# A split between streamed and gathered value columns, moved from 1536 and 512 to 1408 and 640

## The chip, the cores and the metric

The kernel runs on one core of one Trainium2 chip. The metric is the device time of one execution, in microseconds (us).

## What is computed

The kernel is one layer of a decoder: a mixer (a gated recurrence and a convolution side by side) and then an expert layer. The change lies in the second half of the expert layer. There are 256 tokens of width 2048 and 16384 experts, each with a row of `u_table` and a row of `v_table`. Each token has chosen 128 experts (8 heads, 16 each).

```python
u = jnp.take(u_table, ib, axis=0)
act = jnp.einsum('cd,chkd->chk', hb, u)
w = gb * jax.nn.gelu(act)
v = jnp.take(v_table, ib, axis=0)
out = jnp.einsum('chk,chkd->cd', w, v)     # (tokens, 2048)
x = x + gt2[:, None, :] * rms_norm(out, g_post_ffn[l])
```

## The kernel before

The stages follow one another: the mixer, the scores and the first expert product, a short stage that turns the chosen experts into a dense matrix of weights `S` (16384 experts by 256 tokens), and from about 1305 us the value stage, in which `out` is formed.

The 2048 columns of `v_table` are formed in two ways. The first `DV` = 1536 columns are streamed for all experts: the loop over `r` = 0 to 127 takes 128 experts at a time, and `vload` (L1080) loads their 128 x 1536 value rows on SP's queue into one of the three buffers of `vfR`. For float32 precision each operand is split into a high and a low part: `split` (L94) copies on ScalarE (L95, the high part) and subtracts on VectorE (L96, the low part). The high parts go round three buffers (`vHr`), the low parts round two (`vLr`). The load buffer is free again once the low part is formed. `wsplit` (L1050) splits the weights of the next row in the same way, 128 x 256. `vmul` (L1087) then runs 3 products x 2 token halves x 3 blocks of 512 columns, so 18 matmuls a row, into six banks of PSUM.

The last `GV` = 512 columns are gathered for the chosen experts alone: there are 256 units (token half, choice), and for each of them `vgather` (L1062) issues on GpSimd's queue an indirect DMA of 128 rows of 512 columns; `vadd` (L1069) multiplies by the token's weight and adds to `og` on VectorE (L1074; the first of a token half is L1072). A gather buffer returns to the list `gvs` when its addition is issued, and the freed buffer is then gathered into again. The list starts with four buffers (two each in the slots `h2` and `l2`); at rows 7 and 15 the weight rows already used give four more each. Additions start at row 3 (`VLAG`): three a row up to row 8, then two.

VectorE's order in this loop is the written one: `vload`'s low split, `wsplit`'s, then the additions. The other engines' instructions are ordered by the scheduler, with loads and splits moved ahead of their places (`HPV`). SP's queue and GpSimd's queue run in order, as each engine does.

The stage before it (L921 to L1038) shares the area `R` of 28 KB a partition with the value stage's buffers. `trs` and two of the `rawR` buffers lie in it from 10 to 16 KB; `gated` (L968) reads `trs` up to the end of the scores, `weigh` (L990) and `sides` up to the end of that stage. Of the three load buffers, given out from the top down, the first two lie above what these use, the third over it. After the last row the two token halves are normalised, scaled, added to `x1` and written, in four blocks of 512 columns (L1140 to L1162).

Of the kernel before, what the change touches and what calls it, by code (L numbers as in the profile page):

```python
# [11 lines left out]
F32 = mybir.dt.float32  # L12
F32R = mybir.dt.float32r
# [5 lines left out]
PSUM = bass.MemoryType.PSUM  # L19
DRAM = bass.MemoryType.DRAM  # L20

T = 256
D = 2048
# [22 lines left out]
RB = 8  # L46
QPARTS = ((0, 6), (6, 12), (12, 16))
MANV = {mybir.EngineType.DVE}
RKB = 28
# [20 lines left out]
KU = DU // 128  # L70
GU = D - DU
KSL = (6, 6, 4)
DV = 1536
GV = D - DV
UPARTS = ((0, 6), (6, 12))

PCOLS = {}
# [10 lines left out]
def build(nc, tc, A, stop=None):  # L88
    ctx = ExitStack()
    pool = lambda name, bufs=1, **kw: tc.tile_pool(name=name, bufs=bufs, **kw)  # L90
# [45 lines left out]
    def slot(tag, kb, dt=F32):  # L136
        return slots.tile([128, kb * 256], dt, tag=tag, name=f"s{tag}")
# [44 lines left out]
    sb = Area(0, 12, slot("b", 12, F32R))  # L182
# [205 lines left out]
    for j in range(4):  # L388
        n = 0
# [229 lines left out]
    def flat(a, n):  # L619

        return Sf[:, a * T:(a + n) * T]
# [4 lines left out]

    UW = UPARTS[0][1]
    ua = Area(0, RKB - 9)
    sb = Area(0, 12, slot("b", 12, F32R))
# [79 lines left out]
    asked = [False]  # L709
# [93 lines left out]
    def upiece():  # L803
        if "parts" not in state or not state["parts"]:
            state["r"] = r = urows.pop(0)
            state["parts"] = list(UPARTS)
            state["ps"] = accum()
# [13 lines left out]
    with tc.manual_schedule(engines={mybir.EngineType.DVE}):  # L821
        for h in range(NH):
            if h != 1:
                n = 4 if h == 0 else 2
# [41 lines left out]
    xa = Area(tk0, tk1)  # L866
# [32 lines left out]
    pp = psM.enter_context(pool("ppM", space=PSUM))  # L899
    pG = psM.enter_context(pool("pG", 3, space=PSUM))  # L900
    pW = psM.enter_context(pool("pW", 3, space=PSUM))
    va = Area(0, 10)
    wn = va.t(2, NK)
    og = va.t(2, GV)
    jk2 = va.t(128, dt=BF)
    ss = [va.t(4) for _ in range(2)]
    AtR = Area(0, 4, slot("l2", 4)).ring(8, 128)
    xa = Area(10, RKB)
    vfR = Ring([xa.t(DV) for _ in range(3)][::-1])
    BtR = Area(0, 6, slot("h0", 6)).ring(3, 4, 128)  # L910
    ba = Area(0, 6, slot("h1", 6))
    wts = [[ba.t(128) for _ in range(3)] for tt in range(2)]
# [3 lines left out]
    la = [Area(0, 6, slot(x, 6)) for x in ("l0", "l1")]  # L916
    mr = Ring([x.t(1024) for x in la])
    xiR = Ring([x.t(4, 128) for x in la])
    xoR = Ring([og[:, i, :] for i in range(2)])

    def turn():  # L921

        for tt in range(2):
            for q in range(0, KT, 4):
                xi, xo = xiR(), xoR()
                nc.sync.dma_start(xi, x1t[:, q:q + 4, tt * 128:tt * 128 + 128])
                ps = pm.tile([128, 512], F32, name="pm")
                for i in range(4):
                    nc.tensor.transpose(ps[:, 128 * i:128 * i + 128], xi[:, i, :], ident)
                nc.scalar.activation(xo, ps, AF.Copy)  # L930
                nc.sync.dma_start(x1d[tt, :, 128 * q:128 * q + 512], xo)
                yield

    turns = turn()
    mst = va.t(512)
    mods = modfull(5, lambda: pp.tile([128, 512], F32, name="modps"), lambda: pm.tile([128, 512], F32, name="pm"), mr,
                   lambda: mst, 1024, nc.sync, KSPL)

# [92 lines left out]
    for _ in mods:  # L1031
# [6 lines left out]
    psM.close()  # L1038
    vctx = ExitStack()
    pm = vctx.enter_context(pool("pmV", space=PSUM))  # L1040
    out = [[vctx.enter_context(pool(f"po{i}{n}", space=PSUM)).tile([128, 512], F32, name=f"o{i}{n}")
            for n in range(DV // 512)] for i in range(2)]


    units = [(tt, s_) for tt in range(2) for s_ in range(NK)]
    sb = Area(0, 12, slot("b", 12, F32R))
    vHr = Ring([slot("l0", 6, F32R), sb.t(DV), slot("h0", 6, F32R)])
    vLr = Ring([slot("l1", 6, F32R), slot("h1", 6, F32R)])
    WR = sb.ring(3, 2, T)
    def wsplit(r, a=0, b=T):  # L1050
        ww = WR() if a == 0 else wlast.pop(0)
        if b < T:
            wlast.append(ww)
        with tc.high_priority(offset=HPV):
            split(ww[:, 0, a:b], ww[:, 1, a:b], srow(r)[:, a:b])
        return ww[:, 0, :], ww[:, 1, :]

    wlast = []

    gvs, asked = [v for x in ("h2", "l2") for v in Area(0, 4, slot(x, 4)).ring(2, GV).aps], []  # L1060

    def vgather():  # L1062
        tt, s_ = units.pop(0)
        g = gvs.pop(0)
        nc.gpsimd.indirect_dma_start(out=g, out_offset=None, in_=A["vg"],  # L1065
                                     in_offset=bass.IndirectOffsetOnAxis(ap=ei[:, tt, s_:s_ + 1], axis=0))
        asked.append((g, tt, s_))

    def vadd():  # L1069
        g, tt, s_ = asked.pop(0)  # L1070
        if s_ == 0:
            nc.vector.tensor_scalar(og[:, tt, :], g, wn[:, tt, s_:s_ + 1], None, op0=OP.mult)  # L1072
        else:
            nc.vector.scalar_tensor_tensor(og[:, tt, :], g, wn[:, tt, s_:s_ + 1], og[:, tt, :], op0=OP.mult, op1=OP.add)  # L1074
        gvs.append(g)
# [4 lines left out]
    def vload(r, eng=None):  # L1080
        v, vh, vl = vfR(), vHr(), vLr()
        with tc.high_priority(offset=HPV):
            nc.sync.dma_start(v, A["vd"][r])
            split(vh, vl, v, eng)
        return vh, vl

    def vmul(r, w, v, tts=(0, 1), ns=range(DV // 512)):  # L1087
        (wh, wl), (vh, vl) = w, v
        for a, b in ((wh, vh), (wl, vh), (wh, vl)):
            for tt in tts:  # L1090
                for n in ns:
                    nc.tensor.matmul(out[tt][n], a[:, tt * 128:tt * 128 + 128],  # L1092
                                     b[:, 512 * n:512 * n + 512], start=r == 0 and a is wh and b is vh,
                                     stop=r == NK - 1 and b is vl)


# [2 lines left out]
    with tc.high_priority(offset=HPW):  # L1099
        ws = [wsplit(r, 0, 128) for r in range(2)]  # L1100
        for r in range(2):
            vmul(r, ws[r], vs[r], (0,))
    with tc.manual_schedule(engines=MANV):
        for r in range(2):
            wsplit(r, 128)
        wnext = wsplit(2)
        for r in range(NK):
            if r < 2:
                vmul(r, ws[r], vs[r], (1,))
            else:  # L1110
                v, w = vload(r), wnext
                if r < NK - 1:
                    wnext = wsplit(r + 1)
                if r < NK - 2:
                    vmul(r, w, v)
                else:
                    vs[r - NK], ws[r - NK] = v, w
                if r == NK - 1:
                    for tt in range(2):
                        for n in range(DV // 512):  # L1120
                            for i in range(2):
                                vmul(r - 1 + i, ws[i], vs[i], (tt,), (n,))
            if r == 48:
                nc.sync.dma_start(g2r, g2d.rearrange("k c -> (k c)")[None, :].to_broadcast([128, D]))
                for tt in range(2):
                    nc.sync.dma_start(x1[tt], x1d[tt])
            if r == 8:
                nc.scalar.activation(tab, w[0][:, :1].bitcast(F32), AF.Sqrt, scale=0.0, bias=epsc)
            if r % RB == RB - 1 and r < 16:
                gvs.extend(flat(r - RB + 1 + i, 2)[:, :GV] for i in range(0, RB, 2))  # L1130
            for _ in range(0 if r < VLAG else 3 if r < 3 * VLAG else 2):
                if asked:
                    vadd()
            while gvs and units and r < NK - 1:
                vgather()
# [4 lines left out]
    with tc.manual_schedule(engines=MANV):  # L1140
        for tt in range(2):
            y = flat(48 + 8 * tt, 8)
            s = ss[tt]
            nc.scalar.activation(y[:, DV:], og[:, tt, :], AF.Square, accum_out=s[:, 3:4])
            for n in range(3):
                c = slice(512 * n, 512 * n + 512)
                nc.scalar.activation(y[:, c], out[tt][n], AF.Square, accum_out=s[:, n:n + 1])
            nc.vector.tensor_scalar(s[:, 3:4], s[:, 3:4], s[:, 0:1], s[:, 1:2], op0=OP.add, op1=OP.add)
            nc.vector.tensor_tensor(s[:, 3:4], s[:, 3:4], s[:, 2:3], op=OP.add)
            nc.scalar.activation(s[:, 3:4], s[:, 3:4], AF.Sqrt, bias=epsc, scale=1.0 / D)  # L1150
            nc.vector.reciprocal(s[:, 3:4], s[:, 3:4])
            for n in (3, 0, 1, 2):
                c = slice(512 * n, 512 * n + 512)
                src = out[tt][n] if c.stop <= DV else og[:, tt, :]
                add = nc.vector.tensor_tensor if tt and n < 3 else nc.gpsimd.tensor_tensor
                if tt and n == 3:
                    nc.scalar.activation(y[:, c], src, AF.Copy, scale=s[:, 3:4])
                    nc.gpsimd.tensor_tensor(y[:, c], y[:, c], g2r[:, c], op=OP.mult)
                else:
                    nc.vector.scalar_tensor_tensor(y[:, c], src, s[:, 3:4], g2r[:, c], op0=OP.mult, op1=OP.mult)  # L1160
                add(y[:, c], y[:, c], x1[tt][:, c], op=OP.add)
                nc.sync.dma_start(A["out"][tt * 128:tt * 128 + 128, c], y[:, c])  # L1162
# [40 lines left out]
```

## Time and profile before

| | us |
|---|---|
| median of 3 runs | 1884.22 |
| lowest, highest | 1877.45, 1885.96 |
| the profiled execution's own time | 1884.01 |
| its span, first to last instruction | 1882.0 |

| engine | busy, share of the span |
|---|---|
| TensorE | 1795.1 us, 95% |
| VectorE | 1523.8 us, 81% |
| ScalarE | 958.5 us, 51% |
| GpSimd | 786.7 us, 42% |

The profile is of one execution, and its span is 2 us shorter than the time of that execution. Busy time is that of the whole span; the value stage has its own shares. In the rows, PE is TensorE's matmuls, PEld its weight loads, DVE is VectorE, ACT ScalarE, POOL GpSimd, and SPq the queue of SyncE. An engine that sat idle before an instruction has that time and the releaser in brackets. `R`, `S`, `sb`, `sh` and `sl` are the names of areas that several tiles share: `R<-in_vd_dram` is a value load, `sl<-R`, `sb<-R` and `sh<-R` with 1536 columns are its splits, and `S`, `sh` and `sl` with `in_vg_dram` are gather buffers.

### The profile page before, as it was taken

The page shows a single profiled execution, that of the slowest core. Times are in us where ns is not written, and L with a number is a line of the kernel's source. Part 1 is how long each engine was busy: PE and PEld are TensorE (multiplying, and loading weights), DVE is VectorE, ACT ScalarE, POOL GpSimd, SP SyncE. Part 2 cuts the span into 40 slices and gives each one's busy share as a digit, 9 for nine tenths or more (in the row PEclk, how much of TensorE's full clock was granted, in tenths as well). Part 3 has the DMA queues.
Part 4 walks back from the last instruction along what each step waited for, and adds up shares of the span by engine and source line. Part 5 has one row for each costly group of instructions (what it writes and reads, how often), then busy time and mean ns, then how long its engine had stood idle before and what let it go on. Part 6 is the DMA issues. An engine that isn't in the chain of part 4 may idle for free.

```text
span 1882.0 us, 34335 instructions
## 1 busy us (share of the span) xinstructions
PE 1795.1 (95%) x11978; PEld 1544.5 (82%) x11978; DVE 1523.8 (81%) x3946; ACT 958.5 (51%) x1474; POOL 786.7 (42%) x789
## 2 busy tenths in 40 slices
PE   6999999999899999999999998998999999999996
PEld 2667777787899999999999997887777787778774
DVE  3349998755789999999877777999788888888887
ACT  3243333743665555555555558884444444544443
POOL 0000000000035555324555635997776566666662
PEclk8999999999999999999999999999999999999998
DMA  8998889796779989878999886552799889898884
GB/s 311 372 358 277 295 301 322 254 332 249 258 248 302 297 298 300 277 248 288 306 306 305 283 294 200 177 146 80 276 317 335 322 318 313 310 313 313 311 299 155
DMA packets 174652, 530.03 MB, mean 282 GB/s; under 512 B 20736, under 2 KB 44304, under 8 KB 167056
## 3 DMA queue, kind: packets, MB, share of 16 engines
q1 hardware_dynamic: 132656, 391.50, 61.9%
q0 software_dynamic: 40960, 134.25, 19.9%
q8 instruction: 94, 1.54, 0.3%
q10 hardware_dynamic: 864, 2.10, 0.3%
q14 instruction: 78, 0.64, 0.1%
HBM read 521.40 MB, written 6.37 MB: 280 GB/s over the span
## 4 chain that ended last, share of the span: by engine, by line
PE 51%; issue 15%; POOL 14%; DVE 10%; DMA 9%; ACT 2%; SPq 0%; POOLq 0%; ACTq 0%; DVEq 0%
PE acc L788 11%; PE acc L790 11%; PE acc L792 11%; POOL S L1065 7%; DMA PF<-in_w_in_dram 4%; PE acc L354 3%; PE acc L355 3%; PE acc L357 3%; POOL sh L988 3%; PE modps L279 2%; DMA R<-in_vd_dram 2%; POOL sl L1065 2%; POOL sh L1065 2%; PE acc L365 1%; DVE PF L435 1%
## 5 line engine op out<-in xcount | busy, mean ns | idle before, releaser
L788 PE MATMUL acc<-sh,sb 128*128 128x256 f32 x1792 | 443.1, 284 | 1.0 <-ACT sb L95 0.5
L790 PE MATMUL acc<-sl,sb 128*128 128x256 f32 x1768 | 438.9, 284 | 0.4 <-DVE sl L563 0.4
L788 PEld LDWEIGHTS acc<-sh,sb 128*128 128x128 f32 x1792 | 342.6, 192 | 3.4 <-ACT sh L557 2.2
L790 PEld LDWEIGHTS acc<-sl,sb 128*128 128x128 f32 x1768 | 339.3, 192 | 0.6 <-DVE sl L563 0.6
L95 ACT ACTIVATE sb<-R 128x768 fp32r<-128x768 f32 (+2 forms) x203 | 197.1, 971 | 230.0 <-PE acc L790 113.1
L96 DVE TENSOR_TENSOR sb<-S,sb 128x768 fp32r<-128x768 f32 (+3 forms) x274 | 219.0, 800 | 97.0 <-ACT sb L95 84.0
L726 POOL DMA_INDIRECT R<-in_ug_dram,ei x119 | 130.7, 1099 | 386.2 <-ACT gt L705 253.3
L95 ACT ACTIVATE sb<-S 128x768 fp32r<-128x768 f32 (+3 forms) x274 | 207.3, 758 | 115.3 <-PE acc L790 89.4
L792 PE MATMUL acc<-sh,sb 128*128 128x256 f32 x1792 | 264.8, 283 | 0.0
L1065 POOL DMA_INDIRECT S<-in_vg_dram,ei x158 | 214.7, 1359 | 115.6 <-DVE R L1074 84.5
L792 PEld LDWEIGHTS acc<-sh,sb 128*128 128x128 f32 x1792 | 237.1, 192 | 0.0
L1092 PE MATMUL o<-sl,sb 128*128 128x512 f32 x900 | 222.5, 394 | 12.1 <-DVE sl L96 9.4
L1092 PE MATMUL o<-sh,sb 128*128 128x512 f32 x888 | 218.4, 394 | 11.5 <-DVE sh L96 10.2
L726 POOL DMA_INDIRECT S<-in_ug_dram,ei x137 | 153.4, 1120 | 167.4 <-DVE ei L714 97.1
L1092 PEld LDWEIGHTS o<-sl,sb 128*128 128x128 f32 x900 | 166.4, 188 | 57.2 <-DVE sl L96 18.9
L1092 PEld LDWEIGHTS o<-sh,sb 128*128 128x128 f32 x888 | 166.2, 189 | 54.0 <-DVE sh L96 17.8
L96 DVE TENSOR_TENSOR sb<-R,sb 128x768 fp32r<-128x768 f32 (+1 forms) x160 | 150.1, 938 | 51.9 <-ACT sb L95 40.2
L988 POOL TENSOR_SCALAR sh<-iot,R 128x128 f32<-128x128 f32 x248 | 144.8, 602 | 35.3 <-ACT R L892 21.1
L1092 PE MATMUL o<-sb 128*128 128x512 f32 x516 | 126.3, 390 | 0.5 <-ACT sb L95 0.5
L1074 DVE SCALAR_TENSOR_TENSOR R<-S,R 128x512 f32<-128x512 f32 x157 | 117.5, 748 | 3.5 <-DMA S<-in_vg_dram,ei 0.7
L95 ACT ACTIVATE PR<-PF 128x1024 fp32r<-128x1024 f32 (+2 forms) x81 | 66.2, 826 | 95.7 <-DMA PF<-in_w_in_dram 57.5
L1092 PEld LDWEIGHTS o<-sb 128*128 128x128 f32 x516 | 96.7, 188 | 21.2 <-ACT sb L95 0.9
(291 smaller groups left out, 3331.7 us busy)
## 6 DMA issues: line engine op xcount, KB each, us to landing
R<-in_vd_dram SPq DMA_DIRECT2D x128, 768.0 KB
PF<-in_w_mod_dram SPq DMA_DIRECT2D x86, 1024.0 KB
R<-in_ud_dram SPq DMA_DIRECT2D x132, 384.0 KB
S<-in_ud_dram SPq DMA_DIRECT2D x124, 384.0 KB
PF<-in_w_in_dram SPq DMA_DIRECT2D x44, 512.0 KB
PF<-in_w_out_dram SPq DMA_DIRECT2D x32, 512.0 KB
PF<-in_w_in_dram SPq DMA_DIRECT2D x40, 256.0 KB
sl<-in_w_mod_dram SPq DMA_DIRECT2D x20, 512.0 KB
```

The costliest lines, as they stand in the source:

```text
L95: nc.scalar.activation(h, src, AF.Copy)
L96: (eng or nc.vector).tensor_tensor(l, src, h, op=OP.subtract)
L354: nc.tensor.matmul(ps, h[:, k - k0, :], rh(k), start=first and k == k0, stop=False)
L355: nc.tensor.matmul(ps, h[:, k - k0, :], rl(k), start=False, stop=False)
L726: nc.gpsimd.indirect_dma_start(out=g, out_offset=None, in_=A["ug"], in_offset=bass.IndirectOffsetOnAxis(ap=ei[:, tt, s_:s_ + 1], axis=0))
L788: nc.tensor.matmul(ps, uh[:, k - k0, :], hH(k), start=k == 0, stop=False)
L790: nc.tensor.matmul(ps, uh[:, k - k0, :], hL(k), start=False, stop=False)
L792: nc.tensor.matmul(ps, ul[:, k - k0, :], hH(k), start=False, stop=k == end - 1)
L988: eng.tensor_scalar(Bt[:, i, :], iot, trs[tt][:, 1, b + i:b + i + 1], None, op0=OP.is_equal)
L1065: nc.gpsimd.indirect_dma_start(out=g, out_offset=None, in_=A["vg"], in_offset=bass.IndirectOffsetOnAxis(ap=ei[:, tt, s_:s_ + 1], axis=0))
L1074: nc.vector.scalar_tensor_tensor(og[:, tt, :], g, wn[:, tt, s_:s_ + 1], og[:, tt, :], op0=OP.mult, op1=OP.add)
L1092: nc.tensor.matmul(out[tt][n], a[:, tt * 128:tt * 128 + 128], b[:, 512 * n:512 * n + 512], start=r == 0 and a is wh and b is vh, stop=r == ...
```

## The change

`DV` becomes 1408 and `GV` 640. The streamed columns are now taken in blocks of 512, 512 and 384 (`VN`), in `vmul`, in the PSUM banks and at the end. Each load is 128 x 1408, each gather 128 x 640.

The buffers are laid out anew. All of `R` is one area: the load buffers are 1408 wide and lie lower, and the second of them, given out from 3528 to 4936 floats, now overlaps the last 56 columns of `trs` and the two `rawR` buffers in `R`. A gather buffer `gv0` lies at the top of `R`. The slots `h2` and `l2` hold one gather buffer of 640 each, so that the list starts with three; rows 7 and 15 add three each, in place of four.

```diff
-DV = 1536
+DV = 1408
 GV = D - DV
+VN = ((0, 512), (512, 1024), (1024, DV))
...
-    va = Area(0, 10)
+    va = Area(0, RKB)
     wn = va.t(2, NK)
     og = va.t(2, GV)
     jk2 = va.t(128, dt=BF)
+    mst = va.t(512)
     ss = [va.t(4) for _ in range(2)]
...
-    xa = Area(10, RKB)
-    vfR = Ring([xa.t(DV) for _ in range(3)][::-1])
+    vfR = Ring([va.t(DV) for _ in range(3)][::-1])
+    gv0 = va.t(GV)
...
-    out = [[vctx.enter_context(pool(f"po{i}{n}", space=PSUM)).tile([128, 512], F32, name=f"o{i}{n}")
-            for n in range(DV // 512)] for i in range(2)]
+    out = [[vctx.enter_context(pool(f"po{i}{n}", space=PSUM)).tile([128, b - a], F32, name=f"o{i}{n}")
+            for n, (a, b) in enumerate(VN)] for i in range(2)]
...
-    gvs, asked = [v for x in ("h2", "l2") for v in Area(0, 4, slot(x, 4)).ring(2, GV).aps], []
+    gvs, asked = [Area(0, 4, slot(x, 4)).t(GV) for x in ("h2", "l2")] + [gv0], []
...
                     nc.tensor.matmul(out[tt][n], a[:, tt * 128:tt * 128 + 128],
-                                     b[:, 512 * n:512 * n + 512], start=r == 0 and a is wh and b is vh,
+                                     b[:, VN[n][0]:VN[n][1]], start=r == 0 and a is wh and b is vh,
...
             if r % RB == RB - 1 and r < 16:
-                gvs.extend(flat(r - RB + 1 + i, 2)[:, :GV] for i in range(0, RB, 2))
+                gvs.extend(Area(0, RB, flat(r - RB + 1, RB)).ring(RB * T // GV, GV).aps)
...
             for n in (3, 0, 1, 2):
-                c = slice(512 * n, 512 * n + 512)
+                c = slice(*(VN + ((DV, D),))[n])
```

## Rows read from the trace of the kernel before

**Rows 1.** Busy us by stage: PE, PEld, DVE, ACT, POOL; clock, DMA share, GB/s.

```profile
1540.00:1820.00 280.00, 275.76 (x1192) 221.51 (x1192) 244.82 (x265) 138.06 (x135) 178.88 (x133) 1.00 0.89 311
```

**Rows 2.** Groups by shape, 1540 to 1820: busy, mean ns, idle before, releasers.

```profile
L95 ACT ACTIVATE sh<-R 128x1536 fp32r<-128x1536 f32 x22 | 32.8, 1491 | 52.2 <-DMA R<-in_vd_dram 46.8 <-PE o L1092 5.3
...
L96 DVE TENSOR_TENSOR sb<-S,sb 128x256 fp32r<-128x256 f32 x66 | 42.9, 650 | 32.2 <-ACT sb L95 32.1
```

**Rows 3.** Order of time, VectorE (start, us): first and last of 67 low splits.

```profile
1538.77 1.75 DVE L96 TENSOR_TENSOR sh<-R,sl 128x1536 fp32r<-128x1536 f32 x1
...
1817.63 1.75 DVE L96 TENSOR_TENSOR sh<-R,sl 128x1536 fp32r<-128x1536 f32 x1
```

**Rows 4.** Order of time, three rows: start, us, engine, instruction, idle before.

```profile
1610.35 1.49 ACT L95 ACTIVATE sl<-R 128x1536 fp32r<-128x1536 f32 x1 [2.71 <-DMA R<-in_vd_dram]
...
1612.61 4.24 PE L1092 MATMUL o<-sl,sb 128*128 128x512 f32 x18
...
1613.01 1.53 DVE L1074 SCALAR_TENSOR_TENSOR R<-S,R 128x512 f32<-128x512 f32 x2
...
1614.46 1.75 DVE L96 TENSOR_TENSOR sh<-R,sl 128x1536 fp32r<-128x1536 f32 x1
...
1618.05 2.88 PE L1092 MATMUL o<-sb 128*128 128x512 f32 x12
...
1622.83 1.49 ACT L95 ACTIVATE sl<-R 128x1536 fp32r<-128x1536 f32 x1 [3.21 <-DMA R<-in_vd_dram]
```

**Rows 5.** Order of time, SP's queue: two issues of value loads.

```profile
1616.27 0.33 SPq L1083 DMA_DIRECT2D R<-in_vd_dram  x1
...
1845.55 0.33 SPq L1083 DMA_DIRECT2D R<-in_vd_dram  x1
```

**Rows 6.** Order of time, end of stage: last gather, a load's split.

```profile
1840.59 1.36 POOL L1065 DMA_INDIRECT S<-in_vg_dram,ei  x1 [0.30 <-issue]
...
1850.09 1.49 ACT L95 ACTIVATE sl<-R 128x1536 fp32r<-128x1536 f32 x1 [0.39 <-DMA R<-in_vd_dram]
```

**Rows 7.** DMA queues, 1540 to 1820: packets, MB, share of 16 engines.

```profile
q1 hardware_dynamic: 9528, 52.00, 54.7%
q0 software_dynamic: 10600, 34.77, 34.1%
```

**Rows 8.** Groups by shape, whole kernel: the same operations at other widths.

```profile
L95 ACT ACTIVATE sb<-R 128x768 fp32r<-128x768 f32 x150 | 126.7, 844 | 129.1 <-PE acc L790 107.4 <-issue 8.5 <-PE acc L792 3.6
...
L96 DVE TENSOR_TENSOR sb<-R,sb 128x768 fp32r<-128x768 f32 x150 | 143.3, 955 | 44.2 <-ACT sb L95 36.0 <-issue 7.0 <-ACT R L846 0.8
...
L435 DVE SCALAR_TENSOR_TENSOR PF<-R,PF 128x256 f32<-128x256 f32 x240 | 107.6, 475 | 1.3
```

**Rows 9.** Order of time, rows 3 to 7: gathers (GpSimd) and additions (VectorE).

```profile
1321.91 0.75 DVE L1074 SCALAR_TENSOR_TENSOR R<-sl,R 128x512 f32<-128x512 f32 x1
...
1323.00 2.15 POOL L1065 DMA_INDIRECT sh<-in_vg_dram,ei  x1 [0.31 <-DVE R L1074]
...
1329.34 0.75 DVE L1074 SCALAR_TENSOR_TENSOR R<-sh,R 128x512 f32<-128x512 f32 x1 [2.99 <-DMA sh<-in_vg_dram,ei]
...
1334.88 2.15 POOL L1065 DMA_INDIRECT sl<-in_vg_dram,ei  x1 [0.31 <-DVE R L1074]
...
1342.63 0.75 DVE L1074 SCALAR_TENSOR_TENSOR R<-sl,R 128x512 f32<-128x512 f32 x1 [4.18 <-issue]
...
1347.06 0.75 DVE L1074 SCALAR_TENSOR_TENSOR R<-sl,R 128x512 f32<-128x512 f32 x1
```

**Rows 10.** Order of time where the value stage begins: splits and `gated`'s addition.

```profile
1295.24 1.47 ACT L95 ACTIVATE sb<-R 128x1536 fp32r<-128x1536 f32 x1
...
1297.53 0.16 DVE L976 TENSOR_TENSOR sh<-sh,R 128x16 f32<-128x16 f32 x1
...
1308.95 1.76 DVE L96 TENSOR_TENSOR sh<-R,sb 128x1536 fp32r<-128x1536 f32 x1 [0.42 <-PE pm L1029]
```

**Rows 11.** Order of time, the kernel's end: GpSimd's last addition.

```profile
1872.36 1.59 POOL L1161 TENSOR_TENSOR S<-S 128x512 f32<-128x512 f32 x1
```

More of the change, by code (lines that the diff above doesn't have):

```diff
@@ L918, in build @@
     xiR = Ring([x.t(4, 128) for x in la])
-    xoR = Ring([og[:, i, :] for i in range(2)])
+    xoR = Ring([og[:, i, :512] for i in range(2)])
     def turn():
@@ L934, in build @@
     turns = turn()
-    mst = va.t(512)
     mods = modfull(5, lambda: pp.tile([128, 512], F32, name="modps"), lambda: pm.tile([128, 512], F32, name="pm"), mr,
@@ L1040, in build @@
     pm = vctx.enter_context(pool("pmV", space=PSUM))
-    out = [[vctx.enter_context(pool(f"po{i}{n}", space=PSUM)).tile([128, 512], F32, name=f"o{i}{n}")
-            for n in range(DV // 512)] for i in range(2)]
+    out = [[vctx.enter_context(pool(f"po{i}{n}", space=PSUM)).tile([128, b - a], F32, name=f"o{i}{n}")
+            for n, (a, b) in enumerate(VN)] for i in range(2)]
     units = [(tt, s_) for tt in range(2) for s_ in range(NK)]
     sb = Area(0, 12, slot("b", 12, F32R))
-    vHr = Ring([slot("l0", 6, F32R), sb.t(DV), slot("h0", 6, F32R)])
-    vLr = Ring([slot("l1", 6, F32R), slot("h1", 6, F32R)])
+    vHr = Ring([slot("l0", 6, F32R)[:, :DV], sb.t(DV), slot("h0", 6, F32R)[:, :DV]])
+    vLr = Ring([slot(x, 6, F32R)[:, :DV] for x in ("l1", "h1")])
     WR = sb.ring(3, 2, T)
@@ L1085, in vload, with vmul @@
         return vh, vl
-    def vmul(r, w, v, tts=(0, 1), ns=range(DV // 512)):
+    def vmul(r, w, v, tts=(0, 1), ns=range(len(VN))):
         (wh, wl), (vh, vl) = w, v
@@ L1119, in build @@
                     for tt in range(2):
-                        for n in range(DV // 512):
+                        for n in range(len(VN)):
                             for i in range(2):
@@ L1145, in build @@
             for n in range(3):
-                c = slice(512 * n, 512 * n + 512)
+                c = slice(*VN[n])
                 nc.scalar.activation(y[:, c], out[tt][n], AF.Square, accum_out=s[:, n:n + 1])
@@ L1152, in build @@
             for n in (3, 0, 1, 2):
-                c = slice(512 * n, 512 * n + 512)
+                c = slice(*(VN + ((DV, D),))[n])
                 src = out[tt][n] if c.stop <= DV else og[:, tt, :]
```

## The prediction

> **What bounds the kernel now.** The diff touches only the value stage, which begins near 1305 us, so I read the views of that stretch alone, in this order: stages, waits, the order of time, the DMA queues. In the stages [rows 1] look at how many engines are nearly full at once: from 1540 to 1820 us TensorE is busy 275.76 of 280 us, VectorE 244.82, and the DMA engines 0.89 of the time. Busy time can't say which of them sets the pace; the waits can.
>
> [rows 2] give the waits of the same stretch. ScalarE's split of a value row waits for that row's load nearly every time; VectorE's split of the weights waits 32.1 us, all for ScalarE, which stands in order behind that split. In the group of splits shown, the one of three that waits longest for TensorE, that is 5.3 us against 46.8 for loads: TensorE holds almost nobody back. So TensorE is fed just in time, and doesn't set the pace.
>
> The pace itself: 67 low splits stand from the first to the last of [rows 3], so 66 rows took 278.86 us, 4.225 us a row. TensorE's 18 matmuls of a row: 18 in a run last 4.24 and 12 last 2.88 us [rows 4], so 6 more cost 1.36, and 18 cost 4.08. It is short of the pace by 0.15 us a row, hidden inside busy time because the ends are modelled.
>
> What sets 4.225 is a loop through the three load buffers (`vfR`). Follow one in [rows 4]: the load of a row lands and ScalarE splits it at 1610.35; its weights split follows on ScalarE and VectorE; then come the two gathered rows' additions at 1613.01, and only then the low split at 1614.46, which frees the buffer. SP issues the next load into it at 1616.27 [rows 5]: 5.92 us on the engines. That load lands when ScalarE starts at 1622.83, 6.56 us later. Three rows are 12.68 us, so landing takes 12.68 - 5.92 = 6.76 us on average. After the last gather, issued at 1840.59, a load issued at 1845.55 [rows 5] is there at 1850.09 [rows 6]: 4.54 us. Gathers that share the DMA engines thus cost a load 2.22 us, and this is what the change makes bigger.
>
> **The change part by part.**
>
> *Matmuls.* Six of the 18 go from 512 to 384 columns. In proportion TensorE falls from 4.08 to 4.08 x 1408/1536 = 3.74 us a row; if the narrow ones cost as much as wide ones it stays at 4.08. Either way it was not the limit and gains nothing by itself.
>
> *Loads and gathers.* From 1540 to 1820 us the load queue moved 52.00 MB in 54.7% of the engines' time, so 339.5 GB/s alone, and the gather queue 34.77 MB in 34.1%, 364 GB/s [rows 7]. A row's load falls from 786 to 721 KB, 2.32 to 2.12 us: landing gains 0.19. Two gathers grow from 524 to 655 KB, 1.44 to 1.80 us. Together 3.76 becomes 3.92 us a row. The 2.22 us that gathers add I take to grow with their bytes, by a quarter: +0.55. It could stay as it is (0), or the pace could grow with the DMA engines' whole demand, 3.92/3.76. I take the middle one because the landing without gathers in [rows 6] shows that their traffic, not the load's own, makes the difference. Landing: +0.36.
>
> A rule of the Trainium skill (DMA: Bandwidth & Descriptors, Queues, rings and completion order) speaks the other way: each DMA engine takes turns between its queues, a packet at a time. By it a load competing throughout would wait for as much gather traffic as its own length, 2.22 + 2 x 2.32 = 6.86 us, which the 6.76 measured agrees with; after the change it would be 6.46 and the kernel would come out at 1878 us (third rival).
>
> *VectorE and ScalarE in the loop.* A 256-wide addition of this kind takes 0.475 us [rows 8], a 512-wide one 0.75 [rows 9], so 1.07 ns a column: 128 more cost 0.137, twice, +0.27 us. The low split takes 1.75 us for 1536 columns [rows 4] and 0.955 for 768 [rows 8]: 128 fewer save 0.13. ScalarE's, 1.491 [rows 2] and 0.844 [rows 8]: 0.11. Net +0.03. VectorE's busy time goes from 244.82/66.3 rows = 3.69 to 3.83 a row, still under the pace.
>
> *The loop.* +0.36 + 0.03 = 0.39 over three buffers is 0.13 us a row. For rows 9 to 127, 119 of them: **+15.6 us**, from -6.4 (gathers' share unchanged: (0.03 - 0.19)/3) to +22.4 (4.225 x 0.0445 a row).
>
> *Gather buffers at the start.* Until row 7 is done there were four; now there are three, and rows 3 to 8 use three each. From the end of row 3's last addition (1321.91 + 0.75) to that of row 7's (1347.06 + 0.75) [rows 9] four rows took 25.15 us, with VectorE waiting 2.99 and 4.18 us for gathers. A gather issued at 1323.00 is added at 1329.34, one at 1334.88 at 1342.63: 6.34 and 7.75, mean 7.05. With as many buffers as additions in a row, every buffer must turn once a row: 7.05, the addition 0.885, and the 0.31 before GpSimd's issue, 8.24 us; four rows 33.0: **+7.8 us**. With the shorter gather and no gap +3.8, with the longer one +10.6.
>
> *More gathers in flight later.* Nine buffers of 640 instead of twelve of 512 hold 4.5 rows' worth, at 4.36 us a row about 20 us; a gather turns in 8.24. Nothing waits there. GpSimd's issue of a gather has no row at 640 wide; if 2.15 us [rows 9] grew by a quarter, two would take 5.4 us a row, but 178.88 us busy in 66.3 rows [rows 1] is 2.70, with a quarter 3.37: below the pace, so nothing.
>
> *The second load.* Its new place overlaps the last columns of what `gated` reads, so it waits for the addition at 1297.53 [rows 10]. It lands 4.35 us after that ends, at 1302.0; the low split that needs it runs at 1308.95. Behind it on SP stand only loads whose buffers come free later. Nothing, then, unless ScalarE's order keeps its split where it stood, at 1295.24: then ScalarE, with the last copies of the weights behind it, stands for up to 6.8 us. I take 0, since the row's user is 7 us away.
>
> *End.* GpSimd's last addition [rows 11] and the multiplication ahead of it go from 512 to 640 columns: a quarter of 1.59 us each, 0 to +0.8, as VectorE's last blocks get narrower; I take +0.4.
>
> Sum: 15.6 + 7.8 + 0.4 = 23.8 us on the profiled 1884.0, which is also the median shown (1884.22): **1908 us**.
>
> **The rivals.**
> 1. TensorE sets the pace after all, and the change is faster. For it: 275.76 busy of 280 and the 5.3 us that ScalarE waits for it. Against it: no queue of finished splits ahead of it. It would decide if landing fell under 3 x 4.08 - 5.92 = 6.32 us. TensorE would then give 0.34 a row, cut by the DMA engines' 3.92: 119 x 0.305 = -36.3, with +8.2 for start and end 1856 us.
> 2. The wider gathers hide in the DMA engines' idle tenth. For it: share 0.89, not 1. Against it: 2.22 us of landing that go when gathers go. -6.4 + 8.2: 1886 us.
> 3. A load in flight yields every second packet to gathers, however many there are. For it: 6.86 against 6.76. Against it: gathers occupy the engines 1.44 of 4.225 us, so they can't be there throughout. Landing -0.39, loop (-0.39 + 0.03)/3 = -0.12, -14.2 + 8.2: 1878 us. This is the rule named above.
> 4. The upper bounds come: the DMA engines' demand sets the pace, +22.4, the start +10.6, ScalarE's stop +6.8, the end +0.8: 1925 us.
>
> **How the numbers follow.** Forecast 0.60, its own range 1896 to 1920; rivals 0.10, 0.12, 0.07, 0.11. Half a percent, 9.4 us, is about what can be told from no change: below 1874.8 is faster, above 1893.6 slower. Faster: rival 1 and a little of rival 3, 0.12. Slower: the forecast nearly whole and rival 4, 0.70. Same: 0.18. The range 1880 to 1924 leaves out rival 1, half of rivals 3 and 4: 0.19.
>
> **What would show it.** Low splits 4.30 to 4.40 us apart after 1540 us; landing near 7.1 us; additions near 0.885 us; TensorE's busy time falling clearly below that of before in the same rows; VectorE idle 3 to 4 us a row for gathers between rows 4 and 7. The prediction is wrong if landing doesn't grow, or if ScalarE now waits for TensorE and low splits come under 4.1 us apart.

## The result

The changed kernel took 1900.87 us (median of 4 runs, 1900.13 to 1902.36); the kernel before, on the same chip, 1882.01 (4 runs, 1877.45 to 1885.96). The ratio is 1.0101, with a 95% interval of 1.0083 to 1.0119: the change costs 16 to 22 us, some 19. The profiled execution took 1900.13 us, its span 1898.4. Of the lines named here each is one higher than before (the additions are L1075, the matmuls L1093, the splits L96 and L97).

Busy us by stage for the kernel after (PE, PEld, DVE, ACT, POOL; clock, DMA share, GB/s), which answers [rows 1]:

```profile
1540.00:1820.00 280.00, 256.95 (x1151) 206.78 (x1149) 244.93 (x256) 126.48 (x130) 172.20 (x128) 1.00 0.90 315
```

TensorE's busy time fell by 19 us in the same 280, and the kernel is slower. No other engine is full in TensorE's place: VectorE is busy for as long as before, the DMA engines 0.90 of the time in place of 0.89.

Groups of the same stretch, kernel after (busy us, mean ns, idle before and releasers), which answer [rows 2]:

```profile
L1093 PE MATMUL o<-sh,sb 128*128 128x512 f32 (+1 forms) x444 | 103.1, 380 | 12.6 <-DVE sh L97 12.6
...
L1075 DVE SCALAR_TENSOR_TENSOR R<-S,R 128x640 f32<-128x640 f32 x85 | 74.8, 880 | 1.5
...
L97 DVE TENSOR_TENSOR sb<-S,sb 128x256 fp32r<-128x256 f32 x64 | 42.3, 661 | 33.6 <-ACT sb L96 33.4
...
L96 ACT ACTIVATE sh<-R 128x1408 fp32r<-128x1408 f32 x21 | 29.0, 1383 | 47.6 <-DMA R<-in_vd_dram 45.5 <-PE o L1093 2.1
```

The chain of waits is that of before: ScalarE's split waits for the load, VectorE's weights split for ScalarE, TensorE now for VectorE's low split. In the group shown ScalarE's wait for TensorE shrank from 5.3 to 2.1 us. An addition of 640 columns takes 880 ns.

One turn of the loop through a load buffer, kernel after, in order of time (start, us); it answers [rows 4, 5]:

```profile
1586.77 1.62 DVE L97 TENSOR_TENSOR sh<-R,sb 128x1408 fp32r<-128x1408 f32 x1
...
1588.45 0.33 SPq L1084 DMA_DIRECT2D R<-in_vd_dram  x1
...
1595.65 1.39 ACT L96 ACTIVATE sb<-R 128x1408 fp32r<-128x1408 f32 x1 [1.85 <-DMA R<-in_vd_dram]
...
1598.21 1.81 DVE L1075 SCALAR_TENSOR_TENSOR R<-S,R 128x640 f32<-128x640 f32 x2
1599.93 1.62 DVE L97 TENSOR_TENSOR sl<-R,sb 128x1408 fp32r<-128x1408 f32 x1
```

The low split of row 61 ends at 1588.39 and frees its buffer; the load into it is there at 1595.65; its low split, row 64's, ends at 1601.55. That is 7.26 us of landing and 5.90 on the engines for three rows. Taken for every row between 1560 and 1820 us, landing (end of a low split to the start of ScalarE's split three rows on) is 7.18 us on average; measured likewise it was 6.77 before. Low splits 62 and 122 start at 1591.35 and 1853.36, so 4.367 us a row, where before the same rows took 4.229.

DMA queues of that stretch, kernel after (packets, MB, share of 16 engines), which answer [rows 7]:

```profile
q1 hardware_dynamic: 9192, 46.02, 46.7%
q0 software_dynamic: 10229, 41.89, 43.1%
```

The gather queue's time a row, 43.1% of 280 us over 280 / 4.367 rows, is 1.88 us, where 1.80 was worked out and 1.44 stood before.

### The profile page after: what moved, and what is told of

Same layout as the page of the kernel before. It is cut to its first block, busy times and chain, and to the rows that moved or that the text cites. A ratio compares the mean times of both kernels' runs of the same rounds, so it can differ in the third digit from the quotient of the medians.

```text
span 1898.4 us, 34320 instructions
## 1 busy us (share of the span) xinstructions
PE 1779.6 (94%) x11978; PEld 1537.0 (81%) x11978; DVE 1541.7 (81%) x3946; ACT 946.2 (50%) x1474; POOL 791.0 (42%) x789
## 4 chain that ended last, share of the span: by engine, by line
PE 55%; DMA 19%; DVE 13%; issue 7%; ACT 3%; POOL 1%; SPq 0%; ACTq 0%; DVEq 0%; POOLq 0%
DMA R<-in_vd_dram 12%; PE acc L789 11%; PE acc L793 11%; PE acc L791 11%; PE acc L355 4%; PE acc L356 3%; PE acc L358 3%; PE modps L280 3%; PE acc L366 3%; DMA PF<-in_w_in_dram 3%; DVE R L1075 3%; DVE sh L97 2%; DVE sl L97 2%; DVE sl L994 2%; ACT sb L96 2%
## 5 line engine op out<-in xcount | busy, mean ns | idle before, releaser
L96 ACT ACTIVATE sb<-R 128x768 fp32r<-128x768 f32 (+2 forms) x203 | 192.4, 948 | 232.6 <-PE acc L791 125.3
L97 DVE TENSOR_TENSOR sb<-S,sb 128x768 fp32r<-128x768 f32 (+3 forms) x274 | 220.2, 804 | 88.9 <-ACT sb L96 87.6
L96 ACT ACTIVATE sb<-S 128x768 fp32r<-128x768 f32 (+3 forms) x274 | 208.3, 762 | 125.0 <-PE acc L791 99.5
L1093 PE MATMUL o<-sl,sb 128*128 128x512 f32 x900 | 216.7, 388 | 31.9 <-DVE sl L97 28.7
L1093 PE MATMUL o<-sh,sb 128*128 128x512 f32 (+1 forms) x888 | 208.4, 382 | 26.2 <-DVE sh L97 25.2
L1093 PEld LDWEIGHTS o<-sl,sb 128*128 128x128 f32 x900 | 165.3, 192 | 73.8 <-DVE sl L97 41.8
L1093 PEld LDWEIGHTS o<-sh,sb 128*128 128x128 f32 x888 | 161.0, 189 | 66.1 <-DVE sh L97 38.4
L97 DVE TENSOR_TENSOR sb<-R,sb 128x768 fp32r<-128x768 f32 (+1 forms) x160 | 150.2, 939 | 53.2 <-ACT sb L96 49.9
L1075 DVE SCALAR_TENSOR_TENSOR R<-S,R 128x640 f32<-128x640 f32 x158 | 139.1, 881 | 3.5 <-DMA S<-in_vg_dram,ei 0.6
L1093 PE MATMUL o<-sb 128*128 128x512 f32 x516 | 120.0, 378 | 0.7 <-ACT sb L96 0.7
L96 ACT ACTIVATE sl<-R 128x1408 fp32r<-128x1408 f32 x43 | 59.4, 1382 | 110.0 <-DMA R<-in_vd_dram 106.3
L96 ACT ACTIVATE PR<-PF 128x1024 fp32r<-128x1024 f32 (+2 forms) x81 | 66.1, 826 | 91.3 <-DMA PF<-in_w_in_dram 55.8
```

Of the source, the lines that this page charges most:

```text
L96: nc.scalar.activation(h, src, AF.Copy)
L97: (eng or nc.vector).tensor_tensor(l, src, h, op=OP.subtract)
```

## The start, and where its loss went

The low splits of rows 3, 8 and 20 in order of time, first of the kernel before, then of the kernel after:

```profile
1317.22 1.74 DVE L96 TENSOR_TENSOR sh<-R,sl 128x1536 fp32r<-128x1536 f32 x1
...
1347.73 1.75 DVE L96 TENSOR_TENSOR sl<-R,sh 128x1536 fp32r<-128x1536 f32 x1
...
1401.73 1.75 DVE L96 TENSOR_TENSOR sl<-R,sh 128x1536 fp32r<-128x1536 f32 x1
```

```profile
1316.48 1.61 DVE L97 TENSOR_TENSOR sh<-R,sl 128x1408 fp32r<-128x1408 f32 x1
...
1337.64 0.89 DVE L1075 SCALAR_TENSOR_TENSOR R<-R 128x640 f32<-128x640 f32 x1 [3.64 <-DMA R<-in_vg_dram,ei]
...
1346.31 0.89 DVE L1075 SCALAR_TENSOR_TENSOR R<-R 128x640 f32<-128x640 f32 x1 [4.01 <-DMA R<-in_vg_dram,ei]
...
1354.70 1.62 DVE L97 TENSOR_TENSOR sl<-R,sh 128x1408 fp32r<-128x1408 f32 x1
...
1402.23 1.62 DVE L97 TENSOR_TENSOR sl<-R,sh 128x1408 fp32r<-128x1408 f32 x1
```

From row 3 to row 8 the kernel after took 38.22 us against 30.51: +7.7, with VectorE waiting for gathers as foreseen (the longest wait of row 5 and that of row 6 are shown). From row 8 to row 20 it took 47.53 against 54.00: 6.5 us came back. From row 20 to row 127 it lost 15.3 again (row 127 starts at 1874.88, before at 1859.11), 0.143 us a row.

Between rows 8 and 20 ScalarE's order is for the most part another. Two stretches of the kernel after in order of time, rows 14, 21 and 22:

```profile
1375.79 1.38 ACT L96 ACTIVATE sh<-R 128x1408 fp32r<-128x1408 f32 x1 [2.60 <-DMA R<-in_vd_dram]
1376.33 0.68 DVE L97 TENSOR_TENSOR sb<-S,sb 128x256 fp32r<-128x256 f32 x1
...
1403.73 1.39 ACT L96 ACTIVATE sl<-R 128x1408 fp32r<-128x1408 f32 x1 [2.02 <-DMA R<-in_vd_dram]
...
1407.76 1.38 ACT L96 ACTIVATE sb<-R 128x1408 fp32r<-128x1408 f32 x1 [2.64 <-DVE sh L97]
1409.04 0.68 ACT L96 ACTIVATE sb<-S 128x256 fp32r<-128x256 f32 x1
1409.76 0.68 DVE L97 TENSOR_TENSOR sb<-S,sb 128x256 fp32r<-128x256 f32 x1 [2.08 <-ACT sb L96]
```

At 1376.33 VectorE splits the weights of the next row without a wait, though that row's load has only just landed: ScalarE had done its part a row earlier. At 1403.73 and 1407.76 ScalarE has two row splits in a row, the weights split comes after the second, and VectorE waits 2.08 us for it. Told apart through the whole stage by counting ScalarE's splits: before, the split of row r stands ahead of the weights split of row r from row 4 to the end (call it the late order); after, it does in rows 4 to 9, 22 to 25 and 27 to 127, while rows 10 to 21 and 26 have the order in which the code is written, weights first. The diff doesn't touch this order; the scheduler laid it out anew.

## The experiments

"Pace" is the time from the start of row 62's low split to that of row 122's, over 60 rows. "Landing" is measured as above, between 1560 and 1820 us.

**1. Shorter gathers in the changed kernel.**

```diff
-        nc.gpsimd.indirect_dma_start(out=g, out_offset=None, in_=A["vg"],
+        nc.gpsimd.indirect_dma_start(out=g[:, :512], out_offset=None, in_=A["vg"],
...
-        "vg": c_(i["peer_v"][0][:, DV:]),
+        "vg": c_(i["peer_v"][0][:, DV:DV + 512]),
```

> The changed kernel with 512 of its 640 gathered columns fetched (the other 128 of each gather buffer are set to zero once, so the output lacks them); load, matmuls and the 640-wide additions stay. Theory (the wider gathers delay the value loads inside the loop of three load buffers): landing falls by about 0.55 us, the row pace by 0.18 us, the kernel to about 1880 us. Rival (the longer additions on VectorE, or the layout, are the cost): within 5 us of the changed kernel's 1901.

Measured: 1875.47 us (1872.86 to 1876.45), ratio to before 0.9953 (0.9936 to 0.9969); pace 4.123 us, landing 6.27. Low splits of rows 62 and 122 of this run:

```profile
1582.09 1.62 DVE L97 TENSOR_TENSOR sl<-R,sh 128x1408 fp32r<-128x1408 f32 x1
...
1829.47 1.62 DVE L97 TENSOR_TENSOR sl<-R,sh 128x1408 fp32r<-128x1408 f32 x1
```

ScalarE's order is that of the changed kernel from row 6 on. The bytes of the gathers alone cost the changed kernel 25 us and 0.24 us a row: the mechanism is the right one, and it is larger than expected, 0.91 us of landing in place of 0.55.

**2 and 3. ScalarE in written order, after and before.** The loop's block, which already held VectorE to the written order, now holds ScalarE too (`MANL` names both engines); the same edit in both kernels.

```diff
-    with tc.manual_schedule(engines=MANV):
+    with tc.manual_schedule(engines=MANL):
```

> The changed kernel with ScalarE's instructions of the value loop in the written order, so that the weights' split of the next row stands ahead of the split that waits for a load. Theory (landing, then the weights' split, then both additions, then the low split are one loop through three buffers): additions and the weights' split leave the loop, the pace falls from 4.40 to between 3.92 and 4.05 us a row, the kernel to 1850 to 1862 us. Rival (the DMA engines' bandwidth sets the pace already): the pace stays above 4.3 us, the kernel within 10 us of 1901.

> The kernel before with the same order on ScalarE. Theory: the loop leaves the path and TensorE's 4.08 us a row is the next bound, so about 15 to 18 us less than before, 1865 to 1869 us; TensorE's low waits vanish and ScalarE begins to wait for TensorE. Rival (DMA bandwidth): within 5 us of before.

Measured: after in written order 1845.07 us (1838.65 to 1846.49), ratio 0.9785 (0.9762 to 0.9809), pace 3.850. Before in written order 1852.96 (1850.45 to 1857.99), ratio 0.9844 (0.9825 to 0.9862), pace 4.080. Both gained more than was expected: after lies 5 us under the range given and its pace under 3.92, and before gained 29 to 31 us, nearly twice the 15 to 18. Busy us by stage, first of after, then of before in written order:

```profile
1540.00:1780.00 240.00, 240.00 (x1127) 205.96 (x1126) 237.01 (x250) 126.46 (x127) 184.39 (x125) 1.00 0.98 360
```

```profile
1540.00:1780.00 240.00, 240.00 (x1061) 198.72 (x1060) 219.57 (x236) 127.17 (x120) 181.45 (x118) 1.00 0.91 323
```

Both rows show TensorE at 240 of 240, and mean different things. After, two rows' 18 matmuls stand without a gap in order of time:

```profile
1557.85 4.00 PE L1093 MATMUL o<-sh,sb 128*128 128x512 f32 x18
1561.69 4.00 PE L1093 MATMUL o<-sl,sb 128*128 128x512 f32 x18
```

A row is 3.84 us of TensorE by their starts, VectorE is busy for 237.01 of 240 us, 3.80 a row, and the DMA engines for 0.98 of the time. All three fill the pace of 3.850 nearly whole; which of them sets it can't be told here. Before, the pace is TensorE's 4.08, and ScalarE waits for it. That wait is in the groups of before in written order, 1540 to 1780:

```profile
L95 ACT ACTIVATE sb<-S 128x256 fp32r<-128x256 f32 x59 | 41.6, 705 | 95.7 <-PE o L1092 95.7
```

In written order the weights split and the additions no longer stand behind a landing. Order of time, after in written order:

```profile
1640.91 1.38 ACT L96 ACTIVATE sb<-R 128x1408 fp32r<-128x1408 f32 x1 [1.46 <-DMA R<-in_vd_dram]
...
1641.80 0.67 DVE L97 TENSOR_TENSOR sb<-S,sb 128x256 fp32r<-128x256 f32 x1
1642.39 1.79 DVE L1075 SCALAR_TENSOR_TENSOR R<-S,R 128x640 f32<-128x640 f32 x2
1642.53 0.78 ACT L96 ACTIVATE sb<-S 128x256 fp32r<-128x256 f32 x1 [0.23 <-PE o L1093]
...
1644.11 1.62 DVE L97 TENSOR_TENSOR sl<-R,sb 128x1408 fp32r<-128x1408 f32 x1
```

The row that lands at 1640.91 needs VectorE only at 1644.11; the split of weights and both additions run meanwhile. A landing is then covered by 3 rows less two splits: 11.55 - 3.0 = 8.55 us, where landing took 7.41. With this order the change does gain: 1845.07 against 1852.96, and the intervals stand apart.

**4. Fewer matmuls in the kernel before.** One of the three products of `vmul` left out, so 12 matmuls a row.

```diff
-        for a, b in ((wh, vh), (wl, vh), (wh, vl)):
+        for a, b in ((wh, vh), (wh, vl)):
```

> The kernel before without the product of the weights' low part and the values' high part, 12 matmuls a row in place of 18 (that product is left out of the output). Theory (TensorE doesn't set the pace): within 5 us of before, low splits still 4.2 us apart. Rival (TensorE's 4.08 us a row set the pace): 15 us or more off.

Measured: 1820.48 us (1817.94 to 1825.17), ratio 0.9667 (0.9647 to 0.9688). The pace is 3.692. That is against the expectation, and it looks like proof that TensorE set the pace. But in this build ScalarE stands in written order, or with the weights still earlier, in every row: the scheduler turned the order round. So it was run once more with the order of before written out.

**5. The same, in the order of before.** `vload` is cut in two, `vcopy` (the load and ScalarE's split) and `vlow` (the low split), so that ScalarE's split of row r+1 is written ahead of the weights split of r+1, and ScalarE held to it:

```diff
-                v, w = vload(r), wnext
+                v, w = vlow(*vnext), wnext
                 if r < NK - 1:
+                    vnext = vcopy(r + 1)
                     wnext = wsplit(r + 1)
```

> Again 12 matmuls a row in place of 18 (the product of the weights' low part and the values' high part is left out of the output), with ScalarE's order of the kernel before written out by hand, since leaving matmuls out had let the scheduler turn that order round. Theory (ScalarE's order ties the loop together, TensorE doesn't set the pace of before): low splits 4.1 to 4.25 us apart, the kernel 1865 to 1884 us. Rival (what the run without those matmuls gained came from TensorE's time): the pace falls to 3.7 us and the kernel to 1820 to 1830 us.

Measured: 1882.5 us (10 runs, 1877.12 to 1887.28), ratio 0.9978 (0.9961 to 0.9995), pace 4.236. Low splits of rows 62 and 122, then busy us by stage, of this run:

```profile
1587.42 1.75 DVE L1096 TENSOR_TENSOR sl<-R,sh 128x1536 fp32r<-128x1536 f32 x1
...
1841.58 1.75 DVE L1096 TENSOR_TENSOR sl<-R,sh 128x1536 fp32r<-128x1536 f32 x1
```

```profile
1540.00:1780.00 240.00, 179.32 (x679) 127.92 (x677) 208.72 (x225) 117.64 (x116) 153.61 (x114) 0.96 0.89 309
```

A third of the matmuls gone, TensorE busy 179 of 240 us, and the time all but that of before (at most 0.4% less); the pace is 4.236, and 4.258 in run 10, which has this order and all the matmuls. (TensorE's granted clock was 0.96 of full speed on average here, and 1.00, so 2.4 GHz, before; it still stood idle for a quarter of the time.) TensorE didn't set the pace of before. What run 4 gained, 63 us, has two parts: the order alone gives 29 to 31 us (run 3), and only then, with TensorE the bound at 4.080, do fewer matmuls give the rest, down to 3.692. There VectorE's own time a row, 244.82 us over 66.3 rows in [rows 1], is as long.

**6. Shorter additions in the changed kernel.**

```diff
-            nc.vector.scalar_tensor_tensor(og[:, tt, :], g, wn[:, tt, s_:s_ + 1], og[:, tt, :], op0=OP.mult, op1=OP.add)
+            nc.vector.scalar_tensor_tensor(og[:, tt, :512], g[:, :512], wn[:, tt, s_:s_ + 1], og[:, tt, :512], op0=OP.mult, op1=OP.add)
...
```

> The changed kernel with 640 columns gathered and only 512 of them added (128 output columns are left out). Theory: two additions shorter by 0.133 us each lie in the loop, so the pace falls by 0.09 us, the kernel by about 10 us to 1891 us, with landing still near 7.1 us. Rival (only the gathers' bytes count): within 3 us of the changed kernel.

Measured: 1893.74 us (9 runs, 1886.12 to 1903.91), ratio 1.0057 (1.0034 to 1.008); pace 4.272, so 0.095 below the changed kernel's, where 0.27 / 3 = 0.09 was worked out; landing 7.07, nearly unchanged. ScalarE is in the late order from row 4 on here, so the whole time isn't a clean difference; against run 9, which has one order too, the pace is 0.080 lower.

**7. Three gather buffers at the start of the kernel before.**

```diff
-    gvs, asked = [v for x in ("h2", "l2") for v in Area(0, 4, slot(x, 4)).ring(2, GV).aps], []
+    gvs, asked = [v for x in ("h2", "l2") for v in Area(0, 4, slot(x, 4)).ring(2, GV).aps][:3], []
```

> The kernel before with three gather buffers at the start in place of four. Theory as predicted (a buffer must turn once a row): row 8 is reached about 8 us later and the kernel ends 8 us later, 1890 to 1892 us. Rival (seen in the changed kernel: what is lost up to row 8 is given back by row 18, since loads land and are split ahead meanwhile): row 8 5 to 9 us later, the kernel within 3 us of before.

Measured: 1889.12 us (10 runs, 1882.63 to 1896.09), ratio 1.0026 (1.0007 to 1.0045), so +1 to +8 us. In the trace rows 3 to 8 took 6.8 us longer than before; of that 4.1 were left at row 20 and 2.6 at row 127, measured from row 3. The loss at the start comes, and part of it goes again in the same order of ScalarE. How much the time keeps, this interval doesn't tell.

**8. A fourth gather buffer, in the changed kernel in written order.** The tile `mst` is done with before the stage and shares its place with the buffer.

```diff
-    gv0 = va.t(GV)
+    gv0, gv1 = va.t(GV), va.t(GV)
+    mst = gv1[:, :512]
...
-    gvs, asked = [Area(0, 4, slot(x, 4)).t(GV) for x in ("h2", "l2")] + [gv0], []
+    gvs, asked = [Area(0, 4, slot(x, 4)).t(GV) for x in ("h2", "l2")] + [gv0, gv1], []
```

> The changed kernel with ScalarE's written order and a fourth gather buffer at the start, which shares its place with a tile that is free by then. Theory: with the order turned round VectorE sets the pace from row 9 on, so the time lost at the start is no longer given back; four buffers save 5 to 8 us against three, 1837 to 1840 us. Rival: no difference from 1845 us, as the loads still catch up.

Measured: 1842.57 us (1841.3 to 1844.2), ratio 0.9779 (0.9756 to 0.9802): the fastest of all, 2.5 us under run 2, but the intervals overlap. Rows 3 to 8 took 6.08 us each in place of 7.46, so 6.9 us less, and measured from row 3 all of it is still there at row 127 (7.9); but in this execution row 3 stood 4.8 us later than in run 2. So in this pair of traces, where no landing sets the pace, the start's loss wasn't given back; that the kernel's time keeps it, the overlapping intervals don't show.

**9 to 11. The late order written out in both kernels, and the changed kernel again.** The edit of run 5's order, with all matmuls.

> The changed kernel with ScalarE's order of the kernel before written out in the loop for every row: the split of row r+1 ahead of the weights split of r+1. In the trace of the changed kernel ScalarE's queue follows this order from row 3 to 8 and from row 26 on (with rows 21 to 24), but rows 9 to 20 stand in written order (weights split first). Theory A, the 7 us lost at the start were given back by row 20 because rows 9 to 20 stand in the other order: here they aren't, apart from some 3 us that the run with three gather buffers and the one with shorter additions also gave back by row 20 in the old order; the low split of row 20 stands 3 to 5 us behind that of the kernel before, measured from row 3's, where the changed kernel had +1.2, and the time is 1903 to 1905 us against the changed kernel's 1901. Theory B, it is given back because loads fill the three buffers while VectorE waits for gathers, whatever the order: row 20 stands 0 to 1.5 us behind, and the time is that of the changed kernel within 1.5 us.

> The kernel before with its own ScalarE order written out in the same way, nothing else. It tells whether writing the order out costs anything by itself (rows 0 to 2 change place a little). Both theories: the time of the kernel before within 3 us (1880 to 1886), rows 62 to 122 at 4.2 to 4.26 us.

> The changed kernel once more, unaltered, on the same chip as the two runs above, for a comparison with the first of them. Both theories: 1899 to 1903 us, low split of row 20 about 1.2 us behind the kernel before, measured from row 3's.

Measured, beside 1881.70 us for the kernel before (17 runs): before with its order written out 1881.10 (1877.64 to 1885.17), ratio 0.9995 (0.998 to 1.001); the changed kernel again 1897.82 (1894.3 to 1903.13), ratio 1.0092 (1.007 to 1.0114); the changed kernel in the late order throughout 1900.68 (1897.7 to 1903.82), ratio 1.0109 (1.0089 to 1.013). Low splits of rows 3, 8, 20, 62 and 122 of the last (here L1097), in order of time, then of rows 62 and 122 of before with its order written out:

```profile
1317.46 1.61 DVE L1097 TENSOR_TENSOR sh<-R,sl 128x1408 fp32r<-128x1408 f32 x1
...
1355.13 1.62 DVE L1097 TENSOR_TENSOR sl<-R,sh 128x1408 fp32r<-128x1408 f32 x1
...
1407.21 1.62 DVE L1097 TENSOR_TENSOR sl<-R,sh 128x1408 fp32r<-128x1408 f32 x1
...
1594.40 1.62 DVE L1097 TENSOR_TENSOR sl<-R,sh 128x1408 fp32r<-128x1408 f32 x1
...
1855.51 1.62 DVE L1097 TENSOR_TENSOR sl<-R,sh 128x1408 fp32r<-128x1408 f32 x1
```

```profile
1585.14 1.75 DVE L1096 TENSOR_TENSOR sl<-R,sh 128x1536 fp32r<-128x1536 f32 x1
...
1840.64 1.75 DVE L1096 TENSOR_TENSOR sl<-R,sh 128x1536 fp32r<-128x1536 f32 x1
```

From row 3, row 8 stands 7.2 us behind the kernel before, and row 20 still 5.2, where the changed kernel had +1.2 and, run again, +1.7. So of the 6.5 us given back by row 20 some 2 come in the late order too (2.8 in run 7, 3.6 in run 6), and the rest came where rows 10 to 21 stand in the other order: the first theory, for this stretch. But the end doesn't follow: at row 127 the late order stands 16.6 us behind, the changed kernel 16.5 and 15.4, and the times of runs 9 and 11 overlap. Between rows 26 and 62 the changed kernel took 4.51 us a row, before 4.31, and the late order 4.38 against 4.34 for run 10. Most of what was saved in rows 10 to 21 was lost again by row 62: between rows 26 and 62 the changed kernel fell 7.1 us further behind before, the late order 2.5. Why, no run tells. The pair with one order, runs 9 and 10, has paces of 4.352 and 4.258 and landings of 6.98 and 6.78 us.

## Why the prediction came out as it did

1908 us were forecast, with 1896 to 1920 as its own range; 1901 came, and 1898 when the changed kernel was run again.

- *TensorE isn't the bound.* Right: a product of six matmuls, now four wide and two narrow, took 1.28 us in place of 1.36 (in written order 3.84 a row against 4.08), between the two ends given, and gained nothing. Run 5 shows it by itself. Rival 1's bound was near all the same: with ScalarE in written order the kernel before falls to exactly the 4.08 that were read from [rows 4], though not by its condition, a landing under 6.32 us.
- *The loop.* Right in its mechanism and nearly in its steady size: +0.138 us a row in rows 62 to 122 (0.136 in the second execution) against 0.13; landing +0.41 against +0.36; additions 880 ns against 885. Between run 9 and run 10, the pair with one order, it is 0.094, with landing +0.20. So that 0.13 was met to 0.01 is in part luck. Two shares of the landing were off and cancelled: the gathers' bytes cost +0.91 (run 1), not +0.55, so that the shorter loads and all else gave back 0.50, not 0.19.
- *The 119 rows.* This is where the sum failed. It charged 15.6 us for rows 9 to 127 on top of a start of 7.8. From row 8 to 127 the kernel after lost 8.8 us (15.77 - 6.97 from the starts of its low splits), run 9 against run 10 9.4. How the missing 6 to 7 us divide differs by the pair. In the kernels as they are, 6.5 us of the start's loss came back between rows 8 and 20, for the most part in rows with the other order, and from row 20 on each row lost 0.143. In the pair with one order the start cost 8.3, only 1.4 of it had come back by row 20, and the term that was too large is the loss a row: 10.9 us over the 107 rows from row 20 on, 0.10 a row. That rows held up find loads that have landed, and that the rows behind them are therefore faster, is argued and not shown.
- *The start.* +7.7 from row 3 to 8, against +7.8. VectorE waited 3.65, 4.34, 4.01 and 2.90 us for gathers in rows 4 to 7, near the 3 to 4 named.
- *The second load.* Nothing, as taken: it was issued at 1296.51, split at 1300.57, and its low split ran at 1307.12. The upper bound of 6.8 us, that ScalarE stands for it, didn't come: the split has a later place among ScalarE's other work and waited 0.17 us.
- *The end.* From the start of row 127's low split to the last instruction 23.5 us against 22.9: +0.6, predicted +0.4.
- *Rival 3* took the landing to fall to 6.46 us by the turns that a DMA engine takes between its queues. It rose to 7.18, and in run 1, where only the gathers' bytes differ, it followed them. What was made there of the rule of the Trainium skill (DMA: Bandwidth & Descriptors, Queues, rings and completion order), a load that yields every second packet to gathers however many there are, isn't borne out; whether the engines take turns packet by packet, no run here tells. *Rival 2*, that the wider gathers hide, falls to the same numbers. *Rival 4*'s upper bounds didn't come: 0.138 us a row and not 0.188, 7.7 at the start and not 10.6, 0.17 for ScalarE and not 6.8.
- *What the prediction missed* is what decided the matter. It took the weights split and the additions behind a landing as given ("ScalarE, which stands in order behind that split"), and didn't ask why ScalarE stands in that order. That order put them into the loop (whether a fourth load buffer would have opened it too, no run tells): by the medians of the runs it cost the kernel before 29 to 31 us and the changed one 53 to 56.

## What to carry to other kernels

Before shortening an engine's work, write down the loop that sets the pace, instruction by instruction, and ask of each whether it must be in it: here the split and additions that stood in it only by an engine's order were worth more than the change. Where a scheduler lays out the order, compare the orders of the two builds before reading a difference of times as the effect of the edit, and write the order out where they differ; run 4 would have told the opposite of run 5. A delay at the start of a pipelined stage need not last in full: of some 7 to 8 us lost here, between 1.4 and 6.5 had come back twelve rows later, depending on the order and the run.

## What the runs showed of the hardware

- GpSimd's issue of a gather hardly grew with the row: 1363 ns on average for 640 columns, 1350 for 512. The time grew at the other end, in the queue's share. Groups of 1540 to 1820 us, of the kernel before, then after:

```profile
L1065 POOL DMA_INDIRECT S<-in_vg_dram,ei x89 | 120.1, 1350 | 70.3 <-DVE R L1074 54.9 <-issue 13.7 <-DVE R L1072 1.8
```

```profile
L1066 POOL DMA_INDIRECT S<-in_vg_dram,ei x86 | 117.2, 1363 | 67.0 <-DVE R L1075 53.2 <-issue 13.1 <-DVE R L1073 0.7
```

- 0.90 of the DMA engines' time and 315 GB/s were no ceiling: with the loop opened the same transfers ran at 0.98 and 360 GB/s, and landing was longer (7.41 us in place of 7.18) while the kernel got faster.
